# Keys in runs of two instead of four, and the last store moved between the loads of the last head

## Chip, cores, metric

One core of one Trainium2 chip. The metric is the device time of one execution in microseconds (us), lower is better. Engines are named as the profile does: PE is TensorE's matmul, PEld its weight load, DVE VectorE, ACT ScalarE, POOL GpSimd, SPq the sequencer that issues transfers. A transfer *lands* when the engine that waits for it may go on. SBUF is the memory that the engines read, PSUM the one that TensorE writes.

## The reference

```python
batch, n_heads, seq, head_dim = 8, 12, 1024, 64      # scores 1024 x 1024 a head, v 1024 x 64
attn = np.exp(scores - scores_max)
attn = attn / (np.sum(attn, axis=-1, keepdims=True) + 1e-8)
return np.matmul(attn, v).astype(np.float32)
```

There are 96 heads. The scores alone are 403 MB, so the kernel is mostly a stream of loads.

## The kernel before

It handles four heads a pass (`AHEAD = 4`), in 24 passes. Each head is eight rows of scores a partition (`R = 8`). For a row: ScalarE takes exponentials (fp32 to fp16), two rows an instruction; TensorE makes eight transposes of 128x128, in which the exponentials are the *weights*; VectorE copies the eight transposes from PSUM to SBUF (`pt`); TensorE multiplies them with v and a column of ones (the sums). VectorE also spreads v to its places and divides by the sums.

v is loaded with 32 consecutive keys of a head in a partition, 32 partitions a head, and is then spread so that keys stay together in runs of `L`. That sets three patterns: ScalarE's reads (runs of L fp32, 128 bytes from run to run), its writes (runs of 32 x L fp16), and the step of a transpose's weights (L fp16).

```python
    EB = 2; G = 4; LAG = 2; AHEAD = 4
    Q = P // AHEAD        # 32
    S = P // Q
    L = 4                 # keys that stay together
    ...
    out_bufs = buffers(sb_pool, 2, [P, T, R, D], FP32, "out_sb")   # one for two heads
    ...
    # ScalarE, for two rows (the last two rows of a pass one by one)
    nc.scalar.activation(
        out=p_nat[:, g : g + rows, :].rearrange("p r (x v) -> p x r v", v=Q * L),
        in_=s_bufs[k][:, r + g : r + g + rows, :].rearrange(
            "p r (i x l) -> p x (r i) l", i=Q, l=L),
        func=EXP,
    )
    p_row = p_nat[:, r % EB, :].rearrange("p (h q l) -> p h l q", q=P, l=L)
    # TensorE, eight a row; VectorE
    nc.tensor.transpose(out=psT[:, c * P : (c + 1) * P],
                        in_=p_row[:, c // L, c % L, :], identity=order16[:])
    copy = nc.vector.tensor_copy(out=pt[:], in_=psT[:])
    # the products follow two rows behind (LAG)
    ...
    # end of the last pass but one: what is loaded for the last pass
    with tc.If(n0 < BH - AHEAD) as cmp2:
        load(AHEAD - 2, BH - 2, (4, 4))              # head 94 in two parts
        load(AHEAD - 1, BH - 1, (2, 2, 2, 1, 1))     # head 95 in five
        store(n0, AHEAD - T)                         # heads 90 and 91
```

Heads count from 0. The store of heads 90 and 91 reads the same output buffer that head 94 writes in the last pass.

The softmax here doesn't subtract the row's maximum and nothing guards it: scores larger than these inputs give would overflow.

## Time and profile before

| | before |
|---|---|
| median (range) of 4 runs | 1066.26 us (1066.01 to 1066.37) |
| span of the trace | 1064.1 us |
| busy: DVE, ACT, PE, PEld | 74%, 69%, 69%, 64% |
| transfers over the span | 434 GB/s |

A line of the groups says: source line, engine, operation, what is written from what, count, then total busy us and mean ns of one, then the engine's idle time before such instructions and what ended it. The main lines of before stand in the prediction below.

### The profile page before, as it was taken

The page shows a single profiled execution, that of the slowest core. Times are in us where ns is not written, and L with a number is a line of the kernel's source. Part 1 is how long each engine was busy: PE and PEld are TensorE (multiplying, and loading weights), DVE is VectorE, ACT ScalarE, POOL GpSimd, SP SyncE. Part 2 cuts the span into 40 slices and gives each one's busy share as a digit, 9 for nine tenths or more (in the row PEclk, how much of TensorE's full clock was granted, in tenths as well). Part 3 has the DMA queues.
Part 4 walks back from the last instruction along what each step waited for, and adds up shares of the span by engine and source line. Part 5 has one row for each costly group of instructions (what it writes and reads, how often), then busy time and mean ns, then how long its engine had stood idle before and what let it go on. Part 6 is the DMA issues. An engine that isn't in the chain of part 4 may idle for free.

```text
span 1064.1 us, 32213 instructions
## 1 busy us (share of the span) xinstructions
PE 734.8 (69%) x12288; PEld 682.6 (64%) x12288; DVE 786.6 (74%) x1589; ACT 735.8 (69%) x432; POOL 48.0 (5%) x31
## 2 busy tenths in 40 slices
PE   2766766767766667677686776767666777667675
PEld 2765765667666667666575665767665667666575
DVE  3776867868768777677786776868768687686777
ACT  3766776666767668586676866667766668676685
POOL 0000000000000000000000000000000000000000
PEclk9888888878889888888888888878889787897989
DMA  9999999999999999999999999999999999999995
GB/s 394 432 420 434 425 433 434 433 434 433 433 432 432 424 439 432 434 429 427 434 431 436 434 432 434 431 435 422 439 432 434 430 426 435 434 432 427 439 427 233
DMA packets 24915, 453.05 MB, mean 426 GB/s; under 512 B 2768, under 2 KB 2768, under 8 KB 9168
## 3 DMA queue, kind: packets, MB, share of 16 engines
q1 hardware_dynamic: 24912, 453.00, 99.2%
q8 instruction: 3, 0.05, 0.0%
HBM read 436.21 MB, written 25.17 MB: 434 GB/s over the span
## 4 chain that ended last, share of the span: by engine, by line
DMA 78%; ACT 13%; PEld 4%; PE 3%; DVE 1%; issue 1%; SPq 0%; ACTq 0%; DVEq 0%
DMA s_nat<-in_scores_dram 78%; ACT p_nat L255 13%; PEld L267 2%; PE psT L267 2%; PEld L145 1%; DVE pt L273 1%; PE psO_whole L145 1%; PE psO L145 1%; SPq L185 0%; DVE out_sb L129 0%; ACTq L255 0%; SPq L197 0%; DVE recip L124 0%; ACTq L227 0%; DVE vones L208 0%
## 5 line engine op out<-in xcount | busy, mean ns | idle before, releaser
L255 ACT ACTIVATE p_nat<-s_nat 128x2048 f16<-128x2048 f32 (+1 forms) x408 | 705.0, 1800 | 226.7 <-DMA s_nat<-in_scores_dram 200.9
L267 PE MATMUL psT<-order,p_nat 128*128 128x128 f16 x6144 | 578.0, 247 | 263.9 <-ACT p_nat L255 256.9
L273 DVE COPY pt<-psT 128x1024 f16<-128x1024 f16 x768 | 515.6, 687 | 199.9 <-PE L267 121.3
L267 PEld LDWEIGHTS <-p_nat 128*128 128x128 f16 x6144 | 449.9, 123 | 291.1 <-ACT p_nat L255 288.8
L145 PEld LDWEIGHTS <-pt 128*128 128x128 f16 x6144 | 303.1, 108 | 84.4 <-DVE pt L273 81.4
L145 PE MATMUL psO<-vones,pt 128*128 128x65 f16 x3072 | 177.9, 202 | 56.2 <-DVE pt L273 52.6
L145 PE MATMUL psO_whole<-vones,pt 128*128 128x65 f16 x3072 | 190.3, 212 | 3.3 <-DVE pt L273 2.9
L208 DVE COPY vones<-v_half 32x512 f16<-32x512 f16 x384 | 109.4, 285 | 23.1 <-POOL v_half L204 6.0
L255 ACT ACT_TABLE_LOAD x24 | 30.8, 1283 | 89.7 <-DMA s_nat<-in_scores_dram 81.7
L204 POOL CAST v_half<-v_sb 128x2048 f16<-128x2048 f32 x25 | 47.3, 1893 | 1002.2 <-DVE vones L208 957.1
L129 DVE TENSOR_TENSOR out_sb<-psO,recip 64x256 f32<-64x256 f32 x192 | 81.2, 423 | 6.1
L129 DVE TENSOR_TENSOR out_sb<-psO_whole,recip 64x512 f32<-64x512 f32 x96 | 66.1, 688 | 3.7 <-DMA out_dram<-out_sb 0.7
L124 DVE RECIPROCAL recip<-psO 128x4 f32<-128x4 f32 x96 | 17.1, 179 | 34.2 <-PE psO L145 17.8
L124 DVE RECIPROCAL recip<-psO_whole 128x8 f32<-128x8 f32 x48 | 9.7, 203 | 4.8 <-PE psT L267 4.0
L71 DVE MEMSET vones<- 128x16 f16 x4 | 0.2, 72 | 0.8 <-PEq L309 0.8
L62 DVE CAST order<-ident 128x128 f16<-128x128 f32 x1 | 0.2, 227 | 0.4 <-POOL ident masks.py:199 0.4
masks.py:199 POOL TENSOR_SCALAR_AFFINE_SELECT ident<-ident 128x128 f32<-128x128 f32 x1 | 0.3, 292 | 0.1
masks.py:197 POOL MEMSET ident<- 128x128 f32 x1 | 0.2, 204 | 0.3 <-POOLq L309 0.3
L309 POOL MEMSET const-float32-0.0<- 128x1 f32 x1 | 0.1, 98 | 0.2 <-issue 0.2
L309 POOL MEMSET const-bfloat16-1.0<- 128x1 bf16 x1 | 0.1, 102 | 0.0
L309 POOL MEMSET const-uint8-127<- 128x1 uint8 x1 | 0.1, 102 | 0.0
L309 POOL MEMSET const-float32-1.0<- 128x1 f32 x1 | 0.1, 98 | 0.0
## 6 DMA issues: line engine op xcount, KB each, us to landing
s_nat<-in_scores_dram SPq DMA_DIRECT2D x96, 4096.0 KB, 35.9
v_sb<-in_v_dram SPq DMA_DIRECT2D x24, 1024.0 KB, 33.0
out_dram<-out_sb SPq DMA_DIRECT2D x48, 512.0 KB, 27.0
s_nat<-in_scores_dram SPq DMA_DIRECT2D x2, 2048.0 KB, 32.8
s_nat<-in_scores_dram SPq DMA_DIRECT2D x3, 1024.0 KB, 32.6
s_nat<-in_scores_dram SPq DMA_DIRECT2D x2, 512.0 KB
```

The lines of the kernel that those rows point to most:

```text
L62: nc.vector.tensor_copy(out=order16[:].rearrange("p (t j) -> p t j", t=T), in_=ident32[:].rearrange("p (j t) -> p t j", t=T),)
L71: nc.vector.memset(vo[:, :, D : D + 2], 1.0)
L124: nc.vector.reciprocal(out=recip, in_=psO[:, :, :, D : D + 1])
L129: nc.vector.tensor_tensor(out=rows.rearrange("j (b g) d -> j b g d", g=G), in0=psO[part, :, :, 0:D], in1=recip[part].to_broadcast([W, last ...
L145: nc.tensor.matmul(out=bank[:, g * M : (g + 1) * M], lhsT=pt[:, c * P : (c + 1) * P], rhs=st["vones"][:, c, 0:M], start=(c == 0), stop=(c ...
L204: nc.gpsimd.tensor_copy(out=v_half[:], in_=v_sb[:])
L208: copy = nc.vector.tensor_copy(out=vones_bufs[k][s * Q : (s + 1) * Q, :, 0:D].rearrange("i (h l) d -> i h l d", l=L), in_=v_half[k * Q : ( ...
L255: nc.scalar.activation(out=p_nat[:, g : g + rows, :].rearrange("p r (x v) -> p x r v", v=Q * L), in_=s_bufs[k][:, r + g : r + g + rows, :] ...
L267: nc.tensor.transpose(out=psT[:, c * P : (c + 1) * P], in_=p_row[:, c // L, c % L, :], identity=order16[:],)
L273: copy = nc.vector.tensor_copy(out=pt[:], in_=psT[:])
L309: nc = _bacc.Bacc("TRN2", target_bir_lowering=False, num_devices=1)
```

## The change

The intent: weights 4 bytes apart in place of 8, so that a transpose's weight load is cheaper; and a store that no longer comes last, so that head 94's output needn't wait for it.

```diff
-    L = 4
+    L = 2
@@
-    def load(k, n, parts=(R,), **cond):
-        r = 0
+    def load(k, n, parts=(R,), r=0, **cond):
@@
                 load(AHEAD - 2, BH - 2, (4, 4))
-                load(AHEAD - 1, BH - 1, (2, 2, 2, 1, 1))
+                load(AHEAD - 1, BH - 1, (4,))
                 store(n0, AHEAD - T)
+                load(AHEAD - 1, BH - 1, (2, 1, 1), 4)
```

## The prediction

> **What bounds the kernel now.** I read the page first, then the busy time by stretches, then the last 30 us engine by engine. The page's 40 slices and its chain that ended last:
>
> ```profile
> PEclk9888888878889888888888888878889787897989
> DMA  9999999999999999999999999999999999999995
> GB/s 394 432 420 434 425 433 434 433 434 433 433 432 432 424 439 432 434 429 427 434 431 436 434 432 434 431 435 422 439 432 434 430 426 435 434 432 427 439 427 233
> ...
> DMA 78%; ACT 13%; PEld 4%; PE 3%; DVE 1%; issue 1%; SPq 0%; ACTq 0%; DVEq 0%
> ```
>
> The DMA row is full in every slice but the last, and the chain is DMA for 78%. The stretches (length, busy PE, PEld, DVE, ACT, POOL, clock, DMA share, GB/s):
>
> ```profile
> 20.00:1020.00 1000.00, 703.78 (x11737) 654.74 (x11735) 748.79 (x1505) 699.11 (x411) 43.55 (x23) 0.84 1.00 432
> 1048.00:1052.20 4.20, 4.09 (x91) 3.85 (x89) 3.40 (x8) 4.11 (x4) 1.90 (x1) 1.00 0.45 184
> 1052.20:1064.10 11.90, 3.00 (x59) 2.32 (x56) 6.44 (x13) 0.02 (x1) 0.00 (x0) 0.79 0.21 88
> ```
>
> For a thousand microseconds transfers run at 432 GB/s with no hole, while no engine reaches 75%. So the kernel is two stages: a **stream** bound by transfers, where faster engines gain nothing, and a **tail** after about 1030 us, where the last scores are in hand or nearly so and the engines set the end. The groups on which the change works:
>
> ```profile
> L255 ACT ACTIVATE p_nat<-s_nat 128x2048 f16<-128x2048 f32 (+1 forms) x408 | 705.0, 1800 | 226.7 <-DMA s_nat<-in_scores_dram 200.9
> L267 PE MATMUL psT<-order,p_nat 128*128 128x128 f16 x6144 | 578.0, 247 | 263.9 <-ACT p_nat L255 256.9
> L267 PEld LDWEIGHTS <-p_nat 128*128 128x128 f16 x6144 | 449.9, 123 | 291.1 <-ACT p_nat L255 288.8
> L145 PEld LDWEIGHTS <-pt 128*128 128x128 f16 x6144 | 303.1, 108 | 84.4 <-DVE pt L273 81.4
> L208 DVE COPY vones<-v_half 32x512 f16<-32x512 f16 x384 | 109.4, 285 | 23.1 <-POOL v_half L204 6.0
> ```
>
> ScalarE idles 226.7 us for scores, TensorE 263.9 us for ScalarE: both have slack. The weight load of a transpose (steps of 8 bytes) is already nearly as short as the one from pt (side by side), 123 against 108 ns.
>
> The end of the tail, in the timeline of VectorE (start, length, what, idle before it and what ended that):
>
> ```profile
> 1050.70 0.69 DVE L273 COPY pt<-psT 128x1024 f16<-128x1024 f16 x1
> 1052.14 1.41 DVE L129 TENSOR_TENSOR out_sb<-psO_whole,recip 64x512 f32<-64x512 f32 x2 [0.74 <-DMA out_dram<-out_sb]
> 1053.57 1.89 DVE L273 COPY pt<-psT 128x1024 f16<-128x1024 f16 x3
> ...
> 1057.07 0.69 DVE L273 COPY pt<-psT 128x1024 f16<-128x1024 f16 x1
> 1058.48 0.18 DVE L124 RECIPROCAL recip<-psO 128x4 f32<-128x4 f32 x1 [0.72 <-PE psO L145]
> 1058.70 0.88 DVE L129 TENSOR_TENSOR out_sb<-psO,recip 64x256 f32<-64x256 f32 x2
> ```
>
> From 1035 us VectorE works without a pause, save the two waits seen here: **0.74 us for a store** and 0.72 us for the last product. ScalarE is done at 1052.2; three copies that could have run stand behind the first wait. So VectorE, not ScalarE or TensorE, sets the end, and that store's landing stands on its path. It is the store of heads 90 and 91, put in the queue behind all loads of head 95; head 94 may not write the same output buffer until it has landed, at 1052.06 us. The final store leaves at 1059.60.
>
> **What the Trainium skill says.**
> - "DMA: Bandwidth & Descriptors", Where 436 GB/s comes from: the ports allow 435.2 GB/s. The trace agrees: 432 over the stream, so there is next to nothing to gain there.
> - "SBUF — State Buffer", Specifications (TRN2), row Cachelines: lines of 16 bytes, at least two hits a line for full bandwidth. Runs of four fp32 give ScalarE four hits on its reads, runs of two give two: just enough by this rule. The trace of before can't test it, as it has no run of two.
> - "ScalarE: Activation LUTs", What ACT_TABLE_LOAD costs: with immediate scale and bias an ACTIVATE takes 186 ns + 0.833 ns an element, 1892 ns for 2048. The trace shows a median of 1897: today's reads cost nothing extra.
> - "TensorE: Matmul & The Clock Gate", Weight-path perf modes: the fast weight load needs 128 weights of a type other than fp32, and takes strided columns. In the last 30 us at full clock both loads are that short: median 113 ns from p_nat, 98 from pt.
>
> **The change, part by part.**
> *Runs of two: TensorE.* Nothing is added or removed; 6144 weight loads read with a step of 4 bytes for 8. If a load's extra time grows with the lines it crosses (64 lines for 128 weights now, 32 then, 16 side by side), 113 falls to about 98 + 15 x (32-16)/(64-16) = 103 ns, an estimate. But transposes start 55 ns apart at full clock, as their 128 moving columns allow (eight in a row take 0.45 us in the chain), and loads overlap that. In the stream the gain is hidden behind transfers; in the tail TensorE waits for VectorE. On the path: 0.
>
> *Runs of two: ScalarE.* The same 2048 elements, read in pairs, written in runs of 64. By the skill's line rule the time stays 1897 ns. On the path: 0. The slack is large: a pass of four heads takes 43.67 us (distance of two table loads in the timeline); less 1.28 for the table load, over 16 activations, that leaves 2.65 us each against a spacing of 1.80. It would have to become 1.47 times as slow before the stream noticed.
>
> *Runs of two: VectorE's spread of v.* 384 copies, same 32x512 elements, runs of 64 in the output as before: 285 ns stays. 0.
>
> *The store between the parts of head 95.* Before, loads of 2, 2, 2, 1, 1 rows, then the store. After: 4 rows, the store, then 2, 1, 1. Landings before, from the trace: both halves of head 94 at 1036.06 and 1040.89, parts of head 95 at 1043.33, 1045.84, 1048.30, about 1049.5 and 1050.75 (when their waiters were let go), the store at 1052.06. So 1 MB takes 2.48 us, half a MB 1.25, and the store 1.31. After, in the same order of bytes: four rows 1045.84, store 1045.84 + 1.31 = 1047.15, two rows 1049.6, one 1050.85, one 1052.1.
> - The store lands some 4 us before head 94's output needs its buffer (VectorE reaches it at 1051.43, after the copy that ends at 1051.40). The wait of 0.74 falls to the usual 0.03: **-0.71 us** on the path.
> - The loads come later. ScalarE: rows 0-1 start at 1045.95, not 1044.6; 2-3 end at 1049.6; 4-5 at 1051.55; row 6 at 1052.5; row 7 at 1053.5, against 1052.2 now. A row's copy can follow about 0.7 us after its activation (transposes 0.45, latency). Needed by VectorE: row 0 at 1049.34 (ready 1048.5), row 2 at 1050.70 (ready 1050.3), row 4 at 1054.18 - 0.71 = 1053.47 (ready 1052.3), row 6 at 1054.76 (ready 1053.2), row 7 at 1057.07 - 0.71 = 1056.36 (ready 1054.2). VectorE's backlog covers each; the least margin is row 2's 0.4 us. Cost: 0.
> - The branch issues seven transfers in place of eight; the sequencer is not on the path.
>
> In the built program the order of instructions on TensorE, VectorE and GpSimd is the same in both kernels, apart from what that output write waits for; so nothing else moves.
>
> Sum: 1066.23 - 0.71 = 1065.52.
>
> **The rivals.**
> *ScalarE pays for pairs.* If two elements a line are not enough, an activation gets longer. For it: two is the edge of the rule, and nothing in this trace measures it. Against it: the rule as stated. At 1.2 times, the stream doesn't notice, but the tail from 1030 is twelve activations long: 12 x 0.36 = 4.3 us more on ScalarE, of which VectorE's backlog hides perhaps half, so about 1067 to 1068. At double, ScalarE becomes the bound: 16 x 3.6 + 1.28 = 59 us a pass, over 1400 us. I give this 4% in all, 3% for slower by over 2%.
>
> *A wait takes the place of the one removed.* Row 2's margin is small; should the four rows land 0.5 us late, VectorE waits 0.1 us. The later loads could also move the wait to row 7. This would leave a gain of 0 to 0.5 us: 1065.7 to 1066.2. For it: a 2 MB load lands as a whole, so ScalarE loses the early start at 1043. Against it: the margins above.
>
> *TensorE was the bound after all.* If the weight loads held up the whole, 6144 x 10 ns = 61 us could go. Against it: transfers are full for 1000 us at 432 GB/s. I give this under 1%.
>
> **Range and chances.** Runs of before lie within 0.36 us. The mechanism gives -0.7; a wait in its stead 0 to -0.5; a slightly slower activation +1; a different phase of the clock gate in the tail (it was full from 1028 to 1059) up to +1; a better one nothing, a slightly earlier stream perhaps -0.5. Hence 1064.5 to 1066.7. Faster by 2% would need 21 us from a tail of 34 us: 1%. Slower by 2% needs ScalarE's pairs: 3%.
>
> **What the changed profile would show.** DMA still full, 432 GB/s in the stream; the ACTIVATE of 128x2048 at 1.90 us (over 2.0 and the line rule fails here); weight loads from p_nat near 103 ns at full clock with the same time; VectorE's wait for the store gone and no wait of over 0.2 us before the copies of the last head; ScalarE's end about 1.3 us later. A new wait for scores on VectorE's path, or a longer activation, would make the prediction wrong.

## More of the kernel before

A line of waits says: who waited for whom, us in total, times, longest.

One more view is needed later, the waits of the last 30 us (window 1034 to 1064):

```profile
PEld L145 <- DVE pt L273: 6.6, 11, 1.7
...
DVE out_sb L129 <- DMA out_dram<-out_sb: 0.7, 1, 0.7
...
PEld L267 <- ACT p_nat L255: 0.7, 1, 0.7
```

TensorE waits mostly for VectorE's copies there, hardly for ScalarE, and VectorE once for the store.

## The result

| | before | after |
|---|---|---|
| median of 4 runs | 1066.26 us | 1065.89 us |
| range | 1066.01 to 1066.37 | 1065.77 to 1065.96 |
| span of the trace | 1064.08 us | 1063.88 us |

Ratio 0.9997, 95% interval 0.9979 to 1.0014. A ratio is the mean time of one kernel's runs over that of the other's of the same rounds, so not quite the ratio of the medians quoted. The interval is far wider than the 0.37 us between the medians (0.03%); the two ranges don't overlap, but for tenths of a microsecond the argument has to rest on traces.

The page of the changed kernel: transfers, chain, and the groups that the change touches.

```profile
DMA  9999999999999999999999999999999999999995
GB/s 394 432 416 433 430 434 432 433 434 432 434 434 432 423 437 432 430 430 431 434 429 438 434 434 434 429 434 423 437 430 430 434 431 434 434 434 425 442 423 237
...
DMA 80%; ACT 13%; issue 3%; ACTq 1%; PE 1%; DVE 0%; SPq 0%; DVEq 0%
...
L255 ACT ACTIVATE p_nat<-s_nat 128x2048 f16<-128x2048 f32 (+1 forms) x408 | 731.4, 1870 | 207.6 <-DMA s_nat<-in_scores_dram 187.6
...
L267 PEld LDWEIGHTS <-p_nat 128*128 128x128 f16 x6144 | 436.5, 112 | 307.9 <-ACT p_nat L255 304.2
```

The stream is the same. Weight loads got shorter (123 to 112 ns on average), but *activations got longer*: 705.0 to 731.4 us of busy time. With shapes kept apart, one of 128x2048 went from 1901 to 1974 ns. ScalarE pays from its slack: it waited 226.7 us, now 207.6.

The end of VectorE's timeline in the changed kernel:

```profile
1048.92 2.07 DVE L273 COPY pt<-psT 128x1024 f16<-128x1024 f16 x3
1051.02 0.21 DVE L124 RECIPROCAL recip<-psO_whole 128x8 f32<-128x8 f32 x1
1051.26 0.69 DVE L273 COPY pt<-psT 128x1024 f16<-128x1024 f16 x1
1051.98 1.41 DVE L129 TENSOR_TENSOR out_sb<-psO_whole,recip 64x512 f32<-64x512 f32 x2
```

The wait for the store has gone, as forecast. But the copy before the division now starts at 1051.26, not at 1050.70: the three copies take 2.07 us for 1.89, and the reciprocal stands alone. TensorE's timeline shows why (only the lines with a wait, of the same stretch):

```profile
1048.17 0.51 PE L267 MATMUL psT<-order,p_nat 128*128 128x128 f16 x6 [0.65 <-ACT p_nat L255]
...
1050.08 0.40 PE L267 MATMUL psT<-order,p_nat 128*128 128x128 f16 x4 [0.34 <-ACT p_nat L255]
1050.32 0.42 PE L145 MATMUL psO_whole<-vones,pt 128*128 128x65 f16 x8
```

TensorE stood twice for ScalarE, and as its groups come in the same order in every trace here, the last product of head 94 (the line at 1050.32) had to stand behind a transpose of head 95's third row; before, it started at 1049.48. VectorE's reciprocal of head 94 needs it. (By the updates read under experiment 12, only the first of the two stops cost anything.) In the waits of the last 30 us:

```profile
PEld L267 <- ACT p_nat L255: 4.1, 9, 0.8
PEld L145 <- DVE pt L273: 3.6, 7, 1.3
```

Before it was 0.7 and 6.6: TensorE's waiting moved from VectorE to ScalarE.

The balance can be made exact by the instruction times of the traces. Let the mark be the start of VectorE's copy for head 94's last row, and the division the first of the two that write head 94's output.

| kernel | mark to division | division to VectorE's end | wait for the store |
|---|---|---|---|
| before | 3.40 us | 7.44 us | 0.74 us |
| after | 3.06 us | 7.43 us | 0.03 us |

Without any wait the first column is 2.69 us (measured below). So 3.40 is 2.69 + 0.71, and 3.06 is 2.69 + **0.37 us of a new wait**. The net is -0.34 us, close to the -0.37 between the medians. The two spans differ by 0.20 only, as the mark itself came 0.18 us later in this trace; the second half of head 94 landed anywhere between 1040.70 and 1041.20 us in the traces (runs of one aside), so no part of that is put down to the change.

### The profile page after: what moved, and what is told of

Read it like the earlier page. It is cut to its first block, busy times and chain, and to the rows that moved or that the text cites. A ratio compares the mean times of both kernels' runs of the same rounds, so it can differ in the third digit from the quotient of the medians.

```text
span 1063.9 us, 32161 instructions
## 1 busy us (share of the span) xinstructions
PE 730.6 (69%) x12288; PEld 673.8 (63%) x12288; DVE 786.9 (74%) x1589; ACT 762.2 (72%) x432; POOL 48.0 (5%) x31
## 4 chain that ended last, share of the span: by engine, by line
DMA 80%; ACT 13%; issue 3%; ACTq 1%; PE 1%; DVE 0%; SPq 0%; DVEq 0%
DMA s_nat<-in_scores_dram 80%; ACT p_nat L255 13%; PE psT L267 1%; ACTq L255 1%; ACTq L226 0%; PE psO L145 0%; ACTq L292 0%; DVE pt L273 0%; SPq L184 0%; PE psO_whole L145 0%; ACTq L320 0%; DVE out_sb L129 0%; SPq L196 0%; DVE recip L124 0%; ACTq L233 0%
## 5 line engine op out<-in xcount | busy, mean ns | idle before, releaser
L255 ACT ACTIVATE p_nat<-s_nat 128x2048 f16<-128x2048 f32 (+1 forms) x408 | 731.4, 1870 | 207.6 <-DMA s_nat<-in_scores_dram 187.6
L267 PEld LDWEIGHTS <-p_nat 128*128 128x128 f16 x6144 | 436.5, 112 | 307.9 <-ACT p_nat L255 304.2
```

The costliest lines, as they stand in the source:

```text
L255: nc.scalar.activation(out=p_nat[:, g : g + rows, :].rearrange("p r (x v) -> p x r v", v=Q * L), in_=s_bufs[k][:, r + g : r + g + rows, :] ...
L267: nc.tensor.transpose(out=psT[:, c * P : (c + 1) * P], in_=p_row[:, c // L, c % L, :], identity=order16[:],)
```

## Experiments

The theory after the result: the stream hides the runs of two, the store's landing had stood on VectorE's path, and half of what it gave back went into a new wait. Open were the cause of the new wait (the longer activation, or the four rows that land together), the cause of the longer activation, and whether VectorE alone sets the end. Twelve kernels were run.

### 1. Runs of two alone

```diff
-    L = 4
+    L = 2
```

> The runs of two alone, the store last as before. Theory (the tail is VectorE's and the store's landing stands on its path, so a longer activation is hidden): ACTIVATE 128x2048 at about 1974 ns as in the changed kernel, weight loads from p_nat 98 ns, VectorE's wait for the store still 0.5 to 0.75 us, time within 0.2 us of before. Rival (pairs cost time in the tail): 0.4 to 1.0 us longer than before.

Correct; 1066.18 us (1066.08 to 1066.47) against 1066.31 (1066.02 to 1066.73), ratio 0.9999. Activation 1976 ns.

```profile
1052.35 1.41 DVE L129 TENSOR_TENSOR out_sb<-psO_whole,recip 64x512 f32<-64x512 f32 x2 [0.86 <-DMA out_dram<-out_sb]
```

The theory held: ScalarE's last activation ended 0.7 us later than before (1052.94 against 1052.22), and the time didn't move, since the store's landing (1052.27) is waited for anyway. The wait was 0.86, a little over what was expected. The runs of two are worth nothing that shows on their own, and cost nothing that shows.

### 2. The store's place alone

```diff
-                load(AHEAD - 1, BH - 1, (2, 2, 2, 1, 1))
+                load(AHEAD - 1, BH - 1, (4,))
                 store(n0, AHEAD - T)
+                load(AHEAD - 1, BH - 1, (2, 1, 1), 4)    # and load() as in the change
```

> The store's new place alone, runs of four. Theory (of the 0.71 us that the store's wait gave back, 0.37 us went to TensorE standing at head 95's third row for ScalarE, partly as activations are 0.08 us longer): no wait for the store, activation 1.90 us, a new wait on VectorE smaller than in the changed kernel, 0.1 to 0.3 us; time 0.45 to 0.65 us under before. Rival (the new wait comes from the four rows landing together, whatever the activation): time as the changed kernel's, about 0.35 us under before.

Correct; 1065.75 us (1065.65 to 1066.54), ratio 0.9996.

```profile
1048.76 2.04 DVE L273 COPY pt<-psT 128x1024 f16<-128x1024 f16 x3
...
1051.80 1.41 DVE L129 TENSOR_TENSOR out_sb<-psO_whole,recip 64x512 f32<-64x512 f32 x2
```

From mark to division 3.04 us: a new wait of 0.35 us, with activations of 1900 ns. Here my theory missed, though the time is in its range: the new wait is nearly as long as in the changed kernel (0.37), so the longer activation has little part in it. (From the landing of the four rows to the end of the first activation it is 2.09 us in the changed kernel and 2.02 here, so at most 0.07 us.) By the trace the rival was right: it comes from the four rows of head 95 that land together, at 1045.90, where the first two had landed at 1043.33.

### 3. and 4. Six rows, then the store, with runs of four and of two

```diff
-                load(AHEAD - 1, BH - 1, (2, 2, 2, 1, 1))
+                load(AHEAD - 1, BH - 1, (2, 2, 2))
                 store(n0, AHEAD - T)
+                load(AHEAD - 1, BH - 1, (1, 1), 6)
```

> Runs of four; loads of head 95 in 2, 2, 2 rows, the store, 1, 1. Theory: the store lands near 1049.6 us, before VectorE needs its buffer at 1051.4, and rows 0 to 5 land as early as before, so no wait takes its place: 0.65 to 0.75 us under before, ends at about 1063.35. Rival (VectorE isn't the bound of the tail, the gain is given back elsewhere): under 0.4 us.

> The same order of loads, 2, 2, 2, store, 1, 1, with runs of two. Theory (VectorE's backlog covers the longer activations once the rows land early): as the one with runs of four within 0.15 us, 0.55 to 0.75 us under before. Rival (pairs cost time in the tail by themselves): 0.3 us or more behind the one with runs of four.

Both correct. Runs of four: 1065.74 us (1065.19 to 1065.79), ratio 0.9993, span 1063.41. Runs of two: 1065.40 us (1065.29 to 1065.59), ratio 0.9991, span 1063.38. Before in the same rounds: 1066.31 us (1066.02 to 1066.73). From mark to division 2.69 us in both. VectorE with runs of four:

```profile
1050.75 0.69 DVE L273 COPY pt<-psT 128x1024 f16<-128x1024 f16 x1
1051.47 1.41 DVE L129 TENSOR_TENSOR out_sb<-psO_whole,recip 64x512 f32<-64x512 f32 x2
```

The division starts 0.67 us earlier than before (1052.14), with neither wait. With rows 0 to 5 landing as early as before and the store still in time, the whole 0.71 us is kept, with either run length. The median with runs of four falls 0.57 us and misses the 0.65 that was expected, by less than its runs spread; with runs of two it falls 0.91, more than the 0.55 to 0.75 expected, and the two medians lie 0.34 apart where 0.15 was expected, while their traces end within 0.03 us of each other. So a median here is good to some tenths of a microsecond only. This order of loads beats both kernels by their medians (by 0.15 to 0.49 us over the changed kernel's 1065.89, which was timed in other rounds), though not by 2%. Over the store's place alone (1065.75) the times show no gain with runs of four; that the new wait of 0.35 us went is shown by the traces, where VectorE came to the mark at the same time (1048.76, and 1048.78 and 1048.76 here).

### 5. Runs of one

```diff
-    L = 4
+    L = 1
```

> Runs of one, the store last as before: ScalarE reads one fp32 from each line, weights of a transpose lie side by side. Theory A (two hits a line are needed, by the skill's rule): ACTIVATE 128x2048 grows far more than from four to two (73 ns), to 2.6 us or more; over 2.65 us a pass becomes ScalarE's and the time leaves 1066 us, at 3.6 us about 1420 us. Theory B (the pattern costs a little per run, no threshold): about 2.05 to 2.15 us, time still 1066 to 1067 us. Weight loads from p_nat 98 ns either way.

Correct; 1438.23 us, ratio 1.349. Activations by shape, and the page's busy line:

```profile
L255 ACT ACTIVATE p_nat<-s_nat 128x2048 f16<-128x2048 f32 x360 | 1292.9, 3688 | 6.2 <-DMA s_nat<-in_scores_dram 5.9
...
PE 880.8 (61%) x12288; PEld 806.3 (56%) x12288; DVE 807.1 (56%) x1589; ACT 1412.4 (98%) x432; POOL 48.1 (3%) x31
```

Theory A: ScalarE takes twice as long, is busy for 98%, and waits 6.2 us for scores where it had waited 226.7. Four, two and one fp32 in a run cost 1901, 1974 and 3688 ns: two is the last that is nearly free. This is how far the changed kernel stands from a cliff.

### 6. Runs of eight

```diff
-    L = 4
+    L = 8
```

> Runs of eight, the store last as before: two full lines a run for ScalarE, weights of a transpose 16 bytes apart, one a line. ScalarE: 1897 ns as with four (both theories). Weight load at full clock: theory A (time grows with lines crossed) 113 + 15 = 128 to 135 ns; theory B (a threshold of two hits a line, as four weights a line cost nothing and two cost 15 ns) 160 ns or more, then transposes would start over 55 ns apart. Time within 0.5 us of before, as transfers bind the stream.

Correct; 1066.35 us, ratio 1.0002, activations 1901 ns. Weight loads from p_nat at full clock, in the last stretch:

```profile
L267 PEld LDWEIGHTS <-p_nat x137: 142/146/169, 1034.9 to 1051.7; 128*128 128x128 f16 x137
```

The median of 146 ns lies between the two theories, so neither fits. With weights 2, 4, 8 and 16 bytes apart, the loads take 98, 98, 113 and 146 ns (medians at full clock). So the first halving from 8 bytes gains 15 ns and the next nothing. Transposes started 62 ns apart for 56 (medians of the last stretch). Since the time is the same even with these loads, weight loads had nothing to give.

### 7. and 8. Reads or writes

Wrong results; one side of ScalarE's pattern is made plain, in the changed kernel.

```diff
 # read_pairs: the writes (lines joined)
-    out=p_nat[:, g : g + rows, :].rearrange("p r (x v) -> p x r v", v=Q * L),
+    out=p_nat[:, g : g + rows, :],
 # write_short: the reads (lines joined)
-    in_=s_bufs[k][:, r + g : r + g + rows, :].rearrange("p r (i x l) -> p x (r i) l", i=Q, l=L),
+    in_=s_bufs[k][:, r + g : r + g + rows, :],
```

> Wrong result on purpose: the changed kernel with ScalarE reading in pairs as before but writing its 2048 results side by side. Theory A (reads in pairs cost the 73 ns): ACTIVATE 128x2048 stays at 1960 to 1980 ns. Theory B (writes in runs of 64 cost it): back to 1900.

> Wrong result on purpose: the changed kernel with ScalarE reading its rows side by side and writing in runs of 64 as the changed kernel does. Theory A (reads in pairs cost the 73 ns): ACTIVATE 128x2048 at 1895 to 1905 ns. Theory B (writes in runs of 64): 1960 to 1980 ns.

Activations by shape, of the first and of the second:

```profile
L255 ACT ACTIVATE p_nat<-s_nat 128x2048 f16<-128x2048 f32 x360 | 684.7, 1976 | 207.1 <-DMA s_nat<-in_scores_dram 187.3 <-SPq L226 19.5
```

```profile
L255 ACT ACTIVATE p_nat<-s_nat 128x2048 f16<-128x2048 f32 x360 | 658.9, 1899 | 228.8 <-DMA s_nat<-in_scores_dram 202.7 <-SPq L226 25.5 <-PE psT L265 0.2
```

Theory A in both: the reads in pairs cost the 73 ns, the shorter writes nothing.

These two show one thing more. Their loads and store come as in the changed kernel, but VectorE reached the mark later, at 1049.11 us (write_short) and 1049.72 (read_pairs) in place of 1048.92, and from mark to division it took 2.82 and 2.69 us: a new wait of 0.13 and of none. So the 0.37 is no constant of the change. It is what TensorE's lateness exceeds VectorE's own by, and that differs from execution to execution.

### 9. Pairs with a quiet TensorE

Wrong result: in the changed kernel, the second head of each four makes no transposes and one product of eight.

```diff
-                for c in range(C):
+                for c in range(C if k != 1 else 0):
                     nc.tensor.transpose(
@@
-        for c in range(C):
+        for c in range(C if k != 1 else 1):
             nc.tensor.matmul(
@@
-                stop=(c == C - 1),
+                stop=(c == C - 1 or k == 1),
```

> Wrong result on purpose: the changed kernel, where the second head of every four makes no transposes and one product in eight. Theory (reads in pairs have no slack left, so other engines' traffic, TensorE's first, lengthens them; in the changed kernel's trace activations with no weight load beside them average 1946 ns, those with 40 or more 2009): the second heads' activations fall to 1930 to 1950 ns while the others stay near 1975. Rival (the 73 ns are the pattern's alone): second heads as the others, 1970 to 1980 ns.

The stretch of one second head, quiet and in the changed kernel, for the instructions on `p_nat` alone (length, PE, PEld, ACT with counts, clock, DMA share, GB/s):

```profile
462.13:469.64 7.51, 0.52 (x8) 0.34 (x7) 7.50 (x4) 0.79 0.98 424
```

```profile
462.35:469.95 7.60, 4.68 (x63) 3.41 (x60) 7.60 (x4) 1.00 0.97 420
```

Averaged over the first 23 passes, a second head's activations of 128x2048 take 1957 ns quiet against 1987, a little above the 1930 to 1950 expected; the third and fourth of them, when TensorE no longer works off the head before, 1942 against 1988. The other heads hardly change (1966, 1970, 1958 against 1967, 1978, 1960). So in these heads the extra time over 1899 has two parts: near 40 ns that stay with a quiet TensorE, and TensorE's traffic, as much again. With runs of four there is no such dependence: in the trace of before, 90% of the activations lie between 1894 and 1911 ns, where in the changed kernel it is 1943 to 2010.

### 10. and 11. VectorE with less to do

Wrong results: the four copies that spread v for the fourth head are left out, once in the kernel before and once with runs of four and the loads 2, 2, 2, store, 1, 1.

```diff
+        if k == AHEAD - 1:
+            nc.vector.memset(vo[:], 1.0)
@@
-                if k < AHEAD - 1 and r % (R // S) == 0:
+                if k < AHEAD - 2 and r % (R // S) == 0:
                     spread_v(k + 1, r // (R // S), copy)
```

> Wrong result on purpose: the kernel before without the four copies that spread v for the fourth head, so VectorE has 4 x 0.32 = 1.27 us less to do in the tail before it comes to the store's wait. Theory (the store's landing at 1052.06 us stands on the path): the wait grows from 0.74 to about 2.0 us and the time stays, within 0.15 us of before. Rival (VectorE's work alone sets the end): 1.0 to 1.3 us under before.

> Wrong result on purpose: the same four copies left out, with runs of four and the loads 2, 2, 2, store, 1, 1. Theory (with the store landed early, VectorE's work alone sets the end): 0.7 + 1.0 to 1.27 us, so 1.6 to 2.0 us under before. Rival (ScalarE's or the loads' lateness binds as well): 0.7 to 1.2 us under before.

In the kernel before: 1066.18 us (1065.97 to 1066.36), ratio 1.0000. Its VectorE:

```profile
1049.60 0.69 DVE L275 COPY pt<-psT 128x1024 f16<-128x1024 f16 x1 [0.27 <-PE L147]
1050.20 0.20 DVE L126 RECIPROCAL recip<-psO_whole 128x8 f32<-128x8 f32 x1
1050.55 0.69 DVE L275 COPY pt<-psT 128x1024 f16<-128x1024 f16 x1 [0.15 <-PE L147]
1052.39 1.41 DVE L131 TENSOR_TENSOR out_sb<-psO_whole,recip 64x512 f32<-64x512 f32 x2 [1.14 <-DMA out_dram<-out_sb]
```

VectorE had 1.27 us less to do and no time was gained: the store's landing is on the path, as claimed. But the wait for it grew to 1.14 us only, not to 2.0. The rest went into waits for TensorE.

With the store out of the way (less_six): 1065.75 us (1065.06 to 1066.15), ratio 0.9997; span 1063.28 against 1063.41. The mark came 1.12 us earlier, the division only 0.20: from mark to division 3.60 us for 2.69. Theory and rival both failed. **VectorE's work alone does not set the end.** Three copies each stand 0.27 us for TensorE and follow each other every 0.96 us:

```profile
1047.66 0.69 DVE L275 COPY pt<-psT 128x1024 f16<-128x1024 f16 x1 [0.27 <-PE L147]
1048.62 0.69 DVE L275 COPY pt<-psT 128x1024 f16<-128x1024 f16 x1 [0.27 <-PE L147]
```

Yet by the trace TensorE's own instructions had been done well before. The transposes for the copy at 1048.62 ended by 1047.70 (such ends are modelled by the profile; the last of them started at 1047.48). What came late is the *report*: each of TensorE's 24,576 instructions, weight loads too, adds one to a semaphore, and in the trace of before 22,465 of the 24,578 distances between such updates are 30 ns, none under 29. From 1029 to 1054 us there are 807 of them, 24.2 of 25 us. A row of scores takes 16 weight loads and 16 matmuls: 32 x 30 = 0.96 us. That is the spacing of the copies.

The trace files tell more if each update is given to TensorE's instructions in their order. In thirteen of the fourteen traces (all but quiet_pe, which lacks transposes), the copies that had waited over 0.15 us, 3101 in all, start 22 to 25 ns after the update of their row's last transpose, but anywhere from 0.26 to 1.47 us after that transpose's start. And in less_six all 366 distances between updates from 1043 to 1054 us are 30 ns, while transposes start 56 ns apart and products 33. In the trace of before, row 2 of head 95 was copied at 1050.70 us, 0.02 after its update: VectorE had nothing to lend there.

The Trainium skill has this effect for another case: "TensorE: Matmul & The Clock Gate", The cost: per-tile semaphore tail, says that increments at the completion of matmuls serialize, at 26.3 ns each in its fit. The traces here agree that they come one by one, at 30 ns.

### 12. Fewer completions

Wrong result: less_six with half the products.

```diff
-        for c in range(C):
+        for c in range(C // 2):
             nc.tensor.matmul(
@@
-                stop=(c == C - 1),
+                stop=(c == C // 2 - 1),
```

> Wrong result on purpose: as less_six (runs of four, loads 2, 2, 2, store, 1, 1, four spreading copies fewer), and half of the products left out, so TensorE completes 24 instructions a row of scores in place of 32. In less_six, 1.27 us less of VectorE's work gave 0.2 us only: its copies came 0.96 us apart, each 0.27 us late. Theory (TensorE reports its completions one after another, 30 ns each in the traces, so 32 of them cost 0.96 us a row, and that queue is the tail's second limit): with 24 a row, 0.72 us, the 0.27 us waits on copies vanish and the end comes 1.0 to 1.4 us earlier than with less_six by the traces (span 1062.0 to 1062.4 against 1063.3), 1.6 to 2.2 us under before. Rival (something else held the copies, ScalarE or a buffer): span within 0.4 us of less_six.

Both the time and the span fell somewhat more than expected: 1063.60 us (1063.42 to 1064.47) against 1066.21 (1066.03 to 1066.70), ratio 0.9977, 95% interval 0.9963 to 0.9990; span 1061.80.

```profile
1045.46 3.67 DVE L275 COPY pt<-psT 128x1024 f16<-128x1024 f16 x6
...
1056.20 0.18 DVE L126 RECIPROCAL recip<-psO 128x4 f32<-128x4 f32 x1 [0.48 <-PE psO L147]
```

Six copies in a row now take 3.67 us, 0.61 each: the 0.27 us waits have gone. VectorE ends at 1057.30, 1.40 us before less_six; 0.24 of it is the shorter last product (the wait of 0.72 is 0.48), so 1.16 us comes from the freed copies. The rival is out. The run takes away products and their reports together, so it shows that the limit is TensorE's rate by the row; that it is the reports and not the work rests on the traces: at full clock transposes start 56 ns apart and products 33 (medians), so a row's work takes about 8 x 56 + 8 x 33 = 0.71 us by the starts, less than 0.96. No run took away reports and left the work.

This also explains the new wait of the changed kernel. TensorE's reports have almost no slack in the tail, so a pause is not made good: in the changed kernel's trace the updates pause for 0.43 us from 1047.98 (steps of 295 and 139 ns) in place of two usual steps of 30 ns, as the transposes of head 95's first row wait for an activation that ends at 1048.11. That is 0.37 us lost, and the new wait is 0.37. With the store's place alone the pause loses 0.35 us, and the wait is 0.35; with six rows ahead of the store there is no pause, and no wait. TensorE's second stop, at 1050.08, left no pause in the updates. (That pause and wait are one and the same is read from the traces, not tried by itself.)

## Why the prediction was right, and where its steps were not

The time, 1065.89 us, lies in the range 1064.5 to 1066.7, 0.37 us above the 1065.52 predicted. That alone says little: the range also holds the kernel before (1066.26), and the gain came out at half of the 0.71 us predicted. Two of the signs that the prediction itself named as proving it wrong came true, a longer activation and a new wait on VectorE's path; that the wait took no more than half of the gain was not worked out, so there the hit is in part luck. Step by step:

- **The stream hides everything** (right). Transfers still fill each slice, and runs of two alone and runs of eight give the time of before (1066.18 and 1066.35 against 1066.31 and 1066.06 in the same rounds).
- **The wait for the store, -0.71 us** (right in size and cause). It is 0.74 before and 0.03 after; with six rows ahead of the store all 0.71 us shows in the trace, and in less_before taking work off VectorE ahead of the landing gained nothing.
- **"Cost: 0" of the later loads** (wrong). It is 0.37 us. The prediction named row 2 as the least margin, 0.4 us, and used 0.7 us from an activation to its copy. The mis-sized term is that 0.7: in the changed kernel's trace the update of row 2's last transpose came 1.21 us after its activation (1050.03 to 1051.24), and row 0's too (1048.11 to 1049.32). The prediction took a row's transposes as 0.45 us and left out TensorE's order, which puts head 94's last product behind half of row 2's transposes, and its reports, 0.96 us a row. The pause itself fell at row 0, to which the prediction gave a margin of over 0.8 us. So the rival "a wait takes the place of the one removed" came true, and left about half the gain.
- **"VectorE's backlog covers each"; VectorE sets the end** (half right). It is the last in line and has no idle time of its own, but TensorE's reports run only slightly faster than VectorE's work, 0.96 us a row against 8 x 0.69 us of copies and some 3 us of spreading and dividing for eight rows, nearly 1.1 us. So it had little backlog to lend, at row 2 none.
- **The activation stays at 1.90 us** (wrong, without effect). It is 1.97; the slack up to 2.65 us that the prediction worked out is why it didn't matter. In the last 20 us it made ScalarE later, and by the run with the store's place alone this added at most 0.07 us to TensorE's lateness.
- **Weight loads near 103 ns at full clock, time unmoved** (the size off, the conclusion right). They are 98 ns; the estimate by lines crossed doesn't hold, as 4 bytes cost no more than 2. (That such short loads are the skill's fast kind is not shown: no run had the other kind.)
- **ScalarE's end 1.3 us later** (low): 1053.98 against 1052.22, so 1.8, from the longer activations and a stream that was 0.2 us later in this trace.

## What to carry to other kernels

When transfers fill a kernel, look at its last pass only, and ask of each landing there which engine's next instruction needs it: here, half a megabyte moved in one queue was worth more than 6144 cheaper weight loads. When something is moved forward, what stood there moves back: put the store as late as its buffer allows (here after six rows, not four: by the traces 0.35 us), so that no load is late for it. And in a stretch where an engine seems to have backlog to lend, check the engine that feeds it for order and for the rate at which its completions are reported, before calling its cost zero.

## What the Trainium skill lacked or had wrong

- "SBUF — State Buffer", Specifications (TRN2), Cachelines: two hits a line for full bandwidth is nearly right for ScalarE's fp32 reads. Four, two and one in a line took 1901, 1974 and 3688 ns for 2048 elements. It lacks that at two hits the time depends on TensorE's traffic: 1942 ns with TensorE quiet against 1988 (experiment 9).
- The same page and section, for TensorE's weights: eight or four fp16 in a line took 98 ns, but two took 113, so two hits were not enough there; one took 146.
- "TensorE: Matmul & The Clock Gate", The cost: per-tile semaphore tail: it tells the serial increments for packed tiles. It lacks that a plain stream of weight loads and matmuls which all increment is held to one per 30 ns (22,465 of 24,578 distances), which is 0.96 us a row here where the work takes about 0.71 by the starts.
